# Token scaling one product later, half of FF1's input transposed during the last attention block, and a fourth raw place for W1

## The chip, the core and the metric

The kernel runs on one core of one Trainium2 chip. The metric is the device time of one execution in microseconds (us). Its five engines work from queues of their own, each in its program's order: TensorE (PE, matrix products and transposes; PEld is its weight load), VectorE (DVE), ScalarE (ACT), GpSimd (POOL) and SyncE (SP), whose queue issues nearly all DMA transfers. They wait for each other by semaphores.

## The reference

One layer of a decoder trunk on x of 2048 tokens x 1024, all in float32:

```python
a = rms_norm(h, pre_mix_g)
z = a @ w_in                  # 2568 columns: q | k | v | forget logits | u | v_sg
y_att = forgetting_attention(q, k, v, f + f_bias)      # 8 heads of 64, causal
y_sg = chunked_spatial_gating(u_sg, v_sg, ...)         # chunks of 128, 8 groups
y = concat([rms_norm(y_att, att_out_g), rms_norm(y_sg, sg_out_g)])
h = h + rms_norm(y @ w_out, post_mix_g)
c = rms_norm(h, pre_ffn_g)
ff = square(relu(c @ w_ff1)) @ w_ff2                   # 1024 -> 4096 -> 1024
h = h + rms_norm(ff, post_ffn_g)
h = h + sigmoid(h @ ple_gate_w + ple_gate_b) * (p @ ple_w)
```

`rms_norm(x, g)` divides each token by the root of its mean square and multiplies by a gain.

## The kernel before

**Products.** A float32 operand is kept as two parts, a rounded high part and the rest. `mm3` (L102 to L104) makes one product of them from three matrix instructions. ACT writes the high part (`wsp`, `w1p`, `B`: a cast, or an evacuation with a scale, L114), DVE or POOL the low part (L98, L115, L1011). So each operand passes ACT, then DVE or POOL, then PE.

**Input projection** (0 to about 545 us). The tokens are worked in four blocks of 512 (`block(b)`, L346). A block has 24 products: six groups of columns (`GROUPS`) times four. The first three groups give the forget logits, u and v_sg (accumulator `pacc`, evacuated by ACT to `zf` and `ug`, L374, L375), the last three q, k, v (evacuated to `stg`). Behind product number i the `hooks[i]` are called: they load and norm the next block's x. `x_norm` (L292) takes the squares of four token tiles (L303), on POOL the root (L109), and scales x by it (L314). `x_turn` (L316) transposes the scaled x by tiles of 128, one of eight column tiles (kc) behind each of the products 15 to 22, and writes the left operands (`wide`).

**Attention** (about 545 to 1102 us). Blocks b of 512 queries, eight heads in each, so 16 steps per head in the last block b=3, which begins at about 850 us. A step is a pair of score products (L660, L662), the weights on ACT and DVE (`pr`, `hl`), and three products with V (L685 to L687). Between the steps, at rates per step (`Spread`), the output projection of the block before is done (`project(b)`): yT times W_out, the norm of z (L756 to L760), plus x (L763), and the store of the new h into `hS` in DRAM (L764). `hr_all` receives the root for FF1's norm (L771, L772).

**Last projection** (1102 to 1165 us). `project(3)`, four token tiles tt with two halves of 24 products each. Between the products FF1's first input is made: a tile of h (four token tiles times 128 columns, 256 KB) is loaded from `hS` (L1029), multiplied by `hr_all` on POOL (L1030), transposed on PE (L1035), scaled by the gain on ACT. Such tiles go through four places: `v`, `x`, and `ws` twice, called ws0 and ws1 here, plus `px`. `turn` (L1038) stores eight of them to `cS` in DRAM; `join_now` (L1069) joins eight others straight into FF1's right operands `B`. `prep_first` (L1101) strings both together as 16 steps, which a `Filler` spreads over 54 of the projection's ticks; later `join_load` and `join` fetch the stored ones and join them.

**FF1** (1165 to about 1820 us) multiplies by a scheme with seven products of sums of quarter matrices (m = 1 to 7). It runs in units u of 256 columns. `load_w1` (L1131) loads a half unit of W1 (512 KB) into one of three raw places `w1raw`, and `left` (L1182) makes each left operand `w1p` from it: a sum on DVE (L1195, `ws` once more), a cast on ACT (L1008), the low part on DVE (L1011). In `left` the next unit's loads are called for at n = 3 and n = 5 of the seven. The results are stored as `hidC` (L1219). About 1300 us the right operands of the second half are made as well (`prep_next`, `pxn`), stored to `jS` and read back as `B<-jS` at about 1508 us.

**FF2 and the gate** run to the end.

SP's queue works in order. A transfer stands behind each earlier one that still waits: behind `hS<-z` until DVE has made z, behind a load until its place is free.

## Time and profile before

| | us |
|---|---|
| median of 3 runs | 2671.08 (2671.01 to 2671.46) |
| the profiled execution's own time | 2670.59 |
| its span in the trace | 2668.8 |
| PE busy | 2602.6 (98%), 12188 instructions |
| DVE busy | 1803.9 (68%) |
| ACT busy | 1357.6 (51%) |
| POOL busy | 847.7 (32%) |
| mean granted TensorE clock | 0.992 |

A share near 98% for PE says that the rest, 66 us, is in single waits, and only a view of these waits by line says where. The granted clock is a factor on PE's speed: where it is 0.5, a product takes twice its time, and PE counts as busy all the while.

### The profile page before, as it was taken

The page shows a single profiled execution, that of the slowest core. Times are in us where ns is not written, and L with a number is a line of the kernel's source. Part 1 is how long each engine was busy: PE and PEld are TensorE (multiplying, and loading weights), DVE is VectorE, ACT ScalarE, POOL GpSimd, SP SyncE. Part 2 cuts the span into 40 slices and gives each one's busy share as a digit, 9 for nine tenths or more (in the row PEclk, how much of TensorE's full clock was granted, in tenths as well). Part 3 has the DMA queues.
Part 4 walks back from the last instruction along what each step waited for, and adds up shares of the span by engine and source line. Part 5 has one row for each costly group of instructions (what it writes and reads, how often), then busy time and mean ns, then how long its engine had stood idle before and what let it go on. Part 6 is the DMA issues. An engine that isn't in the chain of part 4 may idle for free.

```text
span 2668.8 us, 37153 instructions
## 1 busy us (share of the span) xinstructions
PE 2602.6 (98%) x12188; PEld 2107.5 (79%) x12188; DVE 1803.9 (68%) x3047; ACT 1357.6 (51%) x2678; POOL 847.7 (32%) x823
## 2 busy tenths in 40 slices
PE   8999999999999999989999999999999999999999
PEld 8797879766677777768788788888888888888887
DVE  5445576766778665688788676778786696875443
ACT  7444443348877777655455454455435544453111
POOL 5444443511111110343344223236360171401211
PEclk9999999999999999999999999999999999999999
DMA  6566656497988776455655854448466644673331
GB/s 183 159 185 167 189 154 170 137 223 186 224 205 191 171 194 146 130 179 202 203 194 181 305 170 158 146 153 293 123 207 212 197 151 137 214 248 109 111 119 61
DMA packets 440081, 472.59 MB, mean 177 GB/s; under 512 B 155088, under 2 KB 269520, under 8 KB 439888
## 3 DMA queue, kind: packets, MB, share of 16 engines
q1 hardware_dynamic: 429651, 454.16, 57.9%
q10 hardware_dynamic: 10237, 16.07, 2.2%
q8 instruction: 96, 1.57, 0.3%
q14 instruction: 97, 0.79, 0.1%
HBM read 336.28 MB, written 133.82 MB: 176 GB/s over the span
## 4 chain that ended last, share of the span: by engine, by line
PE 52%; DVE 2%; DMA 2%; issue 1%; POOL 1%; ACT 0%; SPq 0%; DVEq 0%; POOLq 0%; ACTq 0%
PE pf L104 17%; PE pf L103 17%; PE pf L102 17%; DMA w1raw<-in_w_ff_dram 2%; PE pf L1497 1%; DVE w1p L1011 1%; DVE ws L1195 0%; POOL hq L1222 0%; DVE B L1011 0%; PE pf L1035 0%; DMA x<-hS 0%; POOL tmp L1087 0%; DVE hq L1214 0%; DMA cS<-ws 0%; DVE z L763 0%
## 5 line engine op out<-in xcount | busy, mean ns | idle before, releaser
L102 PE MATMUL pf<-B,w1p 128*128 128x512 f32 x752 | 298.1, 397 | 5.9 <-ACT w1p L1008 3.9
L104 PE MATMUL pf<-B,w1p 128*128 128x512 f32 x752 | 296.7, 395 | 5.1 <-DVE w1p L1011 5.0
L1222 POOL TENSOR_TENSOR hq<-hq,hq 128x512 f32<-128x512 f32 x128 | 196.1, 1542 | 329.7 <-ACT hq L1216 294.1
L103 PE MATMUL pf<-B,w1p 128*128 128x512 f32 x752 | 297.3, 395 | 0.0
L673 DVE TENSOR_TENSOR hl<-pr,hl 128x512 fp32r<-128x512 f32 (+1 forms) x320 | 193.4, 616 | 101.8 <-ACT hl L672 85.2
L664 ACT ACTIVATE pr<-pS,bias 128x512 f32<-128x512 f32 (+1 forms) x320 | 194.7, 622 | 86.4 <-PE pS L662 81.6
L98 POOL TENSOR_TENSOR wsp<-wraw,wsp 128x344 fp32r<-128x344 f32 (+1 forms) x176 | 193.0, 1130 | 116.4 <-ACT wsp L94 106.7
L102 PE MATMUL pf<-R,L 128*128 128x512 f32 x452 | 175.9, 389 | 0.0
L104 PE MATMUL pf<-R,L 128*128 128x512 f32 x452 | 175.8, 389 | 0.0
L103 PE MATMUL pf<-R,L 128*128 128x512 f32 x452 | 175.8, 389 | 0.0
L104 PEld LDWEIGHTS pf<-B,w1p 128*128 128x128 f32 x752 | 141.9, 189 | 40.9 <-DVE w1p L1011 8.4
L102 PEld LDWEIGHTS pf<-B,w1p 128*128 128x128 f32 x752 | 141.7, 188 | 40.9 <-ACT w1p L1008 4.3
L103 PEld LDWEIGHTS pf<-B,w1p 128*128 128x128 f32 x752 | 141.7, 188 | 31.6
L102 PE MATMUL pacc<-wsp,wide 128*128 128x344 f32 (+1 forms) x480 | 165.0, 344 | 1.5 <-ACT wide L114 1.5
L672 ACT CAST hl<-pr 128x512 fp32r<-128x512 f32 (+3 forms) x272 | 145.4, 548 | 34.7 <-POOL pr L666 31.2
L103 PE MATMUL pacc<-wsp,wide 128*128 128x344 f32 (+1 forms) x480 | 161.6, 337 | 0.0
L104 PE MATMUL pacc<-wsp,wide 128*128 128x344 f32 (+1 forms) x480 | 161.5, 336 | 0.0
L187 DVE TENSOR_REDUCE mx<-pM 128x1 f32<-128x512 f32 x192 | 129.7, 685 | 41.5 <-PE pM L185 40.8
L1008 ACT CAST L<-lr 128x512 fp32r<-128x512 f32 x113 | 70.3, 622 | 149.8 <-PE pf L103 121.4
L1011 DVE TENSOR_TENSOR L<-lr,L 128x512 fp32r<-128x512 f32 x113 | 96.0, 850 | 69.2 <-ACT L L1008 68.8
L1008 ACT CAST w1p<-w1raw 128x512 fp32r<-128x512 f32 (+1 forms) x123 | 73.3, 598 | 128.3 <-PE pf L103 124.1
L1011 DVE TENSOR_TENSOR w1p<-ws,w1p 128x512 fp32r<-128x512 f32 (+1 forms) x136 | 118.7, 877 | 28.1 <-ACT w1p L1008 26.3
(445 smaller groups left out, 7192.7 us busy)
## 6 DMA issues: line engine op xcount, KB each, us to landing
hidC<-hq SPq DMA_DIRECT2D x224, 256.0 KB
lr<-hidC SPq DMA_DIRECT2D x224, 256.0 KB
w1raw<-in_w_ff_dram SPq DMA_DIRECT2D x64, 512.0 KB
w1raw<-in_w_ff_dram SPq DMA_DIRECT2D x128, 256.0 KB
...
```

The lines of the kernel that those rows point to most:

```text
L98: e.tensor_tensor(dst[:, 1], src, dst[:, 0].bitcast(F32), ALU.subtract)
L102: pe.matmul(ps, l[0], r[0], start=first, stop=False)
L103: pe.matmul(ps, l[0], r[1], start=False, stop=False)
L104: pe.matmul(ps, l[1], r[0], start=False, stop=last)
L187: ve.tensor_reduce(mx[:, tt, c:c + 1], ps, AX.X, ALU.max)
L664: sc.activation(pr[:, off:], ps[:, off:], AF.Exp, bias=bias_of(b)[:, j, h:h + 1])
L672: sc.copy(hl[:, 0, off:], pr[:, off:])
L673: ve.tensor_tensor(hl[:, 1, off:], pr[:, off:], hl[:, 0, off:].bitcast(F32), ALU.subtract)
L1008: sc.copy(dst[:, 0], src)
L1011: (po if lo == "pool" else ve).tensor_tensor(dst[:, 1], src, dst[:, 0].bitcast(F32), ALU.subtract)
L1222: po.tensor_tensor(t, x, y, op)
L1497: pe.transpose(ps[:, kk], hts[t][g][:, kk * P:(kk + 1) * P], ident)
```

## The change

It has three parts. Line numbers below are those of the kernel each list belongs to.

**A.** `x_norm` ends with the root, kept per token tile as `xr0` to `xr3`. The scaling is a function of its own, `x_scale`, called behind the next product, and ordered after that product's evacuation (`tc.issue_after`). For the tiles loaded first DVE scales one half, as before.

**B.** `turns(g)` does the eight transpositions that were stored to `cS` (kc = 2, 6, 3, 7 for two groups of 512 tokens) in the last attention block, one step every five of its steps, through one place `hx` and a PSUM bank that the heads use too. `prep_first` is left with `join_now`, which loads one step ahead through `v`, `x`, ws0 and ws1. It has eight counted steps over 36 ticks; what is left is done at once when they are through. The joins of the stored tiles are spread over 24 ticks, one of them (m = 6) later.

**C.** W1 has a fourth raw place, `w1more`, in which two of the stored tiles lie before, and the next unit's loads are called for at n = 0 and n = 2. `px` gets a place of its own.

```diff
--- before.py
+++ after.py
@@ -111,8 +112,9 @@
 
     def evac_split(dst, ps, scale, lo_out=None):
 
-        sc.activation(dst[:, 0], ps, AF.Copy, scale=scale)
+        hi = sc.activation(dst[:, 0], ps, AF.Copy, scale=scale)
         ve.scalar_tensor_tensor(dst[:, 1], ps, scale, dst[:, 0].bitcast(F32), ALU.mult, ALU.subtract)
+        return hi
 
 
     mph = ExitStack()
...
@@ -304,14 +306,18 @@
                                       accum_out=ss[:, tt, hf:hf + 1])
                 n = t1 - t0
                 ve.tensor_tensor(ss[:, t0:t1, 0], ss[:, t0:t1, 0], ss[:, t0:t1, 1], ALU.add)
-                r = rstd_of(small, ss[:, t0:t1, 0], n, D, "xr")
-                for tt in range(t0, t1):
-                    for hf in range(2):
-                        xh, rt = st["xs"][tt][:, hf * 512:(hf + 1) * 512], r[:, tt - t0:tt - t0 + 1]
-                        if rest is not None and not hf:
-                            ve.tensor_scalar(xh, xh, rt, None, ALU.mult)
-                        else:
-                            sc.activation(xh, xh, AF.Copy, scale=rt)
+                r = st["r", t0] = rstd_of(small, ss[:, t0:t1, 0], n, D, f"xr{t0}")
+                if rest is not None:
+                    x_scale(st, t0, True)
+
+        def x_scale(st, tt, first=False):
+            r = st["r", tt]
+            for hf in range(2):
+                xh = st["xs"][tt][:, hf * 512:(hf + 1) * 512]
+                if first and not hf:
+                    ve.tensor_scalar(xh, xh, r, None, ALU.mult)
+                else:
+                    sc.activation(xh, xh, AF.Copy, scale=r)
 
         def x_turn(st, b, kc, aT):
             ps = ptp.tile([P, 4, P], F32, name="tp")
...
@@ -372,17 +378,18 @@
 
             def fu_done(tt, ps):
                 sc.copy(zf[:, tt], ps[:, :H])
-                sc.activation(ug[:, tt, :336], ps[:, H:344], AF.Gelu_apprx_tanh)
+                return sc.activation(ug[:, tt, :336], ps[:, H:344], AF.Gelu_apprx_tanh)
 
             def qk_done(dst, scale):
...
@@ -493,10 +500,13 @@
                         else:
                             mm3(ps[:, :width], (aT[kc][:, 0, ns], aT[kc][:, 1, ns]),
                                 (wt[kc][:, 0, :width], wt[kc][:, 1, :width]), kc == 0, kc == KC - 1)
-                    dones[gi](n, ps)
+                    evac = dones[gi](n, ps)
                     i = 4 * gi + n
                     for f in mine.get(i, ()):
                         f()
+                    for f in behind.get(i, ()):
+                        with tc.issue_after(evac.ins):
+                            f()
                     for f in hooks.get(i, ()):
                         f()
                     if n == 3 and gi + 1 < len(GROUPS):
...
+            nxt, behind = [], {}
             if b + 1 < NB:
                 box = {}
                 hooks[7].append(lambda: box.update(x_load(b + 1)))
                 for tt in range(4):
                     hooks[XN[tt]].append(lambda tt=tt: x_norm(box, ((tt, tt + 1),)))
+                    behind[XN[tt] + 1] = [lambda tt=tt: x_scale(box, tt)]
                 for kc in range(KC):
                     hooks[15 + kc].append(lambda kc=kc: x_turn(box, b + 1, kc, nxt))
-            block(b, aT, hooks, fill, None if b else (ug0, gv0, wt0))
+            block(b, aT, hooks, behind, fill, None if b else (ug0, gv0, wt0))
             if b < NB - 1:
                 fill.drain()
             aT = nxt
...
@@ -824,9 +836,31 @@
             if not last:
                 yield
 
+    def turns(g):
+
+        t0 = g * 4
+        for kc in (2, 6, 3, 7):
+            hx = yp.tile([P, 4, P], F32, name="hx", bufs=1)
+            sy.dma_start(hx, hS[t0 * P:(t0 + 4) * P, kc * P:(kc + 1) * P].rearrange("(a p) c -> p a c", p=P))
+            po.tensor_tensor(hx, hx, hr_all[:, t0:t0 + 4].unsqueeze(2).broadcast_to([P, 4, P]), ALU.mult)
+            yield
+            ps = pT.tile([P, 4, P], F32, name="pT")
+            for a in range(4):
+                pe.transpose(ps[:, a], hx[:, a], ident)
+            hx = hx.rearrange("p a b -> p (a b)")
+            sc.activation(hx, ps.rearrange("p a b -> p (a b)"), AF.Copy, scale=g_pf[:, kc:kc + 1])
+            sy.dma_start(cS[kc, :, g * 512:(g + 1) * 512], hx)
+            yield
+
+    projected = []
+
+    def project_all(b):
+        yield from project(b)
+        projected.append(b)
+
     YSQ, YNO = 8, 13
     YSQL, YNOL = 2, 7
-    PREPT = 54
+    PREPT, JOINT = 36, 24
     GAP = 2
     FIN = (0, 2)
     LA = 4
     LA = 4
@@ -893,6 +927,7 @@
     lv = Spread(late_v())
     mx3 = Spread(fill.gen, maxima(NB - 1))
     proj = Spread()
+    turned = [Spread(turns(g)) for g in range(2)]
     n3 = m_units(NB - 1)
     m01 = (M3PART * n3 + fill.left) / MEND
     rates = {0: (m01, 0), 1: (m01, 0), 2: ((1 - M3PART) * n3 / 94, P2PARTS / 96),
...
@@ -918,6 +953,7 @@
         if i == 24:
             sy.dma_start(g_att, att_out_g[0].partition_broadcast(P))
             sy.dma_start(g_post, post_mix_g[0].partition_broadcast(P))
+            sy.dma_start(g_pf, pre_ffn_g[0].rearrange("(k p) -> p k", p=P))
         for d, f in ((0, load_wo), (WOH, wo_hi), (WOL, wo_lo)):
             if i - d in WO:
                 f(WO[i - d])
...
         proj.tick(rates[b][1])
+        if b == NB - 1:
+            for g in projected:
+                if g < 2:
+                    turned[g].tick(.2)
     for _ in late[1]:
         pass
+    for t in turned:
+        t.drain()
     aph.close()
     mph.close()
 
...
@@ -970,22 +1012,21 @@
     w1s = ExitStack()
     w1q = pool(w1s, "w1q", side="right")
     pf1 = pool(fps, "pf1", 3, PSUM, side="right")
-    g_pf = per_part(fsm, "g_pf", pre_ffn_g, KC)
     v_t = fsm.tile([P, 512], F32, name="v")
     x_t = fsm.tile([P, 512], F32, name="x")
     ng_pf = fsm.tile([P, KC], F32, name="ng_pf")
     ve.tensor_scalar(ng_pf, g_pf, -1.0, None, ALU.mult)
     ws = [fsm.tile([P, 4, P], F32, name=f"ws{e}") for e in range(2)]
-    px = [*ws, w1q.tile([P, 4, P], F32, name="px")]
 
     def w1_places(pl):
 
         all = pl.tile([P, 3, KC, P], F32, name="w1raw")
-        return all, [all[:, e] for e in range(3)]
+        return all, [all[:, 2], all[:, 0], all[:, 1], w1more]
 
     def w1_pieces(pl):
         return [pl.tile([P, 2, 4, P], F32R, name=f"w1p{e}") for e in range(3)]
 
+    w1more = fsm.tile([P, KC, P], F32, name="w1more")
     _, w1raw = w1_places(w1q)
     w1p = w1_pieces(w1q)
 
@@ -993,7 +1034,7 @@
 
     LATE = (6, 3, 7, 2, 4)
     B = [[None] * KH for _ in range(8)]
-    EARLY = (1, 3, 2, 5, 6)
+    EARLY = (1, 3, 2, 5)
     early = [ctx3.tile([P, 2, 512], F32R, name=f"B{m}_2") for m in EARLY]
     kept = [ctx3.tile([P, 2, 512], F32R, name=f"B{m}_1") for m in LATE]
     for k in range(2):
...
@@ -1066,13 +1097,24 @@
             halves_of(B[m][k], t, "act", "dve")
             yield
 
-    def join_now(k, b, place, done, ra, rd, h1, h2):
+    def join_now(k, b, place, done, ra, rd, hs):
+
 
         t2 = None
-        for n, (hx, dst, jh, l) in enumerate(((h1, ra, 0, 0), (h2, rd, 1, 1), (h1, None, 0, 1), (h2, None, 1, 0))):
+        ahead = len(hs) > 1
+        parts = ((ra, 0, 0), (rd, 1, 1), (None, 0, 1), (None, 1, 0))
+
+        def fetched(n):
+            if n < 4:
+                normed(hs[n % len(hs)], KH * parts[n][1] + k, 2 * b + parts[n][2])
+
+        if ahead:
+            fetched(0)
+        for n, (dst, jh, l) in enumerate(parts):
+            hx = hs[n % len(hs)]
             kc = KH * jh + k
             g, ng = g_pf[:, kc:kc + 1], ng_pf[:, kc:kc + 1]
-            normed(hx, kc, 2 * b + l)
+            fetched(n + ahead)
             yield
             ps = turned(hx)
             if n < 2:
@@ -1099,18 +1141,10 @@
 
 
     def prep_first():
-        pa = w1raw[0].rearrange("p k f -> p (k f)")
-        pb = w1raw[1].rearrange("p k f -> p (k f)")
+        pa = w1raw[1].rearrange("p k f -> p (k f)")
         v4, x4 = (t.rearrange("p (a b) -> p a b", b=P) for t in (v_t, x_t))
-        n = 0
         for k in range(2):
-            now = join_now(k, 0, lambda m: B[m][k], lambda m: None, pa[:, :512], pa[:, 512:], v4, x4)
-            for g in range(2):
-                for kc in (2 + k, 6 + k):
-                    for _ in turn(kc, g, px[n % 3]):
-                        next(now)
-                        yield
-                    n += 1
+            yield from join_now(k, 0, lambda m: B[m][k], lambda m: None, pa[:, :512], pa[:, 512:], [v4, x4, *ws])
 
     def prep_next():
 
...
+
+    pxn = px = None
+    raws, nraw, nleft = {}, 0, 0
     lefts = {}
 
     def load_w1(u, c):
         nonlocal nraw
-        t = w1raw[nraw % 3]
+        t = w1raw[nraw % 4]
         nraw += 1
         f0 = u % NF * FCH + c * P
         sy.dma_start(t, w_ff1[:, f0:f0 + P].rearrange("(k p) f -> p k f", p=P))
         raws[u, c] = t
 
     load_w1(0, 0)
-    pfill = Filler(prep_first(), 16, PREPT)
-    w1raw1 = w1raw[1].rearrange("p k f -> p (k f)")
-    jraw = [w1raw1[:, :512], w1raw1[:, 512:], v_t, px[2].rearrange("p a b -> p (a b)")]
+    pfill = Filler(prep_first(), 8, PREPT)
+    w1raw1 = w1raw[2].rearrange("p k f -> p (k f)")
+    w1more1 = w1more.rearrange("p k f -> p (k f)")
+    jraw = [w1raw1[:, :512], w1raw1[:, 512:], w1more1[:, :512], w1more1[:, 512:]]
     pl = []
     join2 = None
     for n, _ in enumerate(last_proj):
@@ -1147,9 +1182,9 @@
         if not pfill.left and join2 is None:
             pfill.drain()
             join_load(2, jraw)
-            pl += [new_tmp() for _ in range(2)]
+            pl.append(new_tmp())
             join2 = join(2, lambda: pl.pop(0), jraw)
-            jfill = Filler(join2, 5, 10)
+            jfill = Filler(join2, len(EARLY), JOINT)
         elif join2 is not None:
             jfill.tick()
     while jfill.left:
@@ -1200,9 +1235,9 @@
         halves_of(w[:, :, kk], t, "act", "dve")
         lefts[i] = w
         if u + 1 < NU and ks[-1] == 3:
-            if n == 3:
+            if n == 0:
                 load_w1(u + 1, 0)
-            elif n == 5:
+            elif n == 2:
                 load_w1(u + 1, 1)
 
     hq = {}
...
@@ -1382,7 +1418,7 @@
     fill = Filler(prep_next(), 32, 13 * 7)
     jrest = join_rest()
     hold = first_of[NF + 2]
-    JR = (1, 1, 2, 2, 1, 1, 1)
+    JR = (1, 1, 2, 2, 2, 1, 1)
 
     NEXT = [[(1, 2), (1, 3)], [(5, 2), (5, 3)], [(6, 1)], [(3, 1), (6, 2), (6, 3)], [(7, 1), (3, 2), (3, 3)],
             [(2, 1), (7, 2), (7, 3)], [(4, 1), (2, 2), (2, 3), (4, 2), (4, 3)]]
```

`normed` and `turned` are unchanged, but the name `turned` is also that of the list of the two spread generators. ACT in the first block's products (`pacc` to `zf` and `ug`), before:

```order
L303 ACTIVATE junk,xss<-xt 128x512 x5
L374 COPY zf<-pacc 128x8
L375 ACTIVATE ug<-pacc 128x336
L314 ACTIVATE xt<-xt,xr 128x512 x6
L374 COPY zf<-pacc 128x8
L375 ACTIVATE ug<-pacc 128x336
L94 CAST wsp<-wraw 128x512 x4
```

and with the change:

```order
L305 ACTIVATE junk,xss<-xt 128x512
L380 COPY zf<-pacc 128x8
L381 ACTIVATE ug<-pacc 128x336
L95 CAST wsp<-wraw 128x512 x6
L380 COPY zf<-pacc 128x8
L381 ACTIVATE ug<-pacc 128x336
L95 CAST wsp<-wraw 128x512
L402 ACT_TABLE_LOAD
L402 ACTIVATE lse<-lse 128x32
L95 CAST wsp<-wraw 128x512
L115 ACTIVATE stg<-pacc 128x512
L320 ACTIVATE xt<-xt,xr_883 128x512 x2
```

The six scalings that stood ahead of an evacuation now go in pairs, each behind an evacuation to `stg`.

PE where the last projection's third token tile (tile 2) begins, with `pT<-ident,yn` as the mark of that place, before:

```order
L1035 MATMUL pf_12619<-ident,ws_12326 128x128 x4
L1035 MATMUL pf_12626<-ident,v 128x128 x4
L102 MATMUL pM<-wide_118,yaT 128x512
L103 MATMUL pM<-wide_118,yaT 128x512
L104 MATMUL pM<-wide_118,yaT 128x512
L102 MATMUL pM<-wide_120,yaT 128x512
L103 MATMUL pM<-wide_120,yaT 128x512
L104 MATMUL pM<-wide_120,yaT 128x512
L781 MATMUL pT<-ident,yn 128x128 x4
```

and with the change (ws_12405 is ws0, ws_12406 is ws1):

```order
L1076 MATMUL pf_12657<-ident,ws_12406 128x128 x4
L1076 MATMUL pf_12672<-ident,v 128x128 x4
L1076 MATMUL pf_12682<-ident,x 128x128 x4
L793 MATMUL pT<-ident,yn 128x128 x4
L103 MATMUL pW<-wide_126,ysT 128x512
L1076 MATMUL pf_12692<-ident,ws_12405 128x128 x4
L104 MATMUL pW<-wide_126,ysT 128x512
L105 MATMUL pW<-wide_126,ysT 128x512
L103 MATMUL pW<-wide_128,ysT 128x512
L104 MATMUL pW<-wide_128,ysT 128x512
L105 MATMUL pW<-wide_128,ysT 128x512
L1076 MATMUL pf_12709<-ident,ws_12406 128x128 x4
```

SP's queue ahead of it, with the change:

```order
L1070 DMA v<-hS 128x4x128
L741 DMA ysT<-ysS 128x1024
L1070 DMA x<-hS 128x4x128
L776 DMA hS<-z_12512 128x512
L776 DMA hS<-z_12536 128x512
L819 DMA xt_12596<-in_x_dram 128x512
L819 DMA xt_12621<-in_x_dram 128x512
L1070 DMA ws_12405<-hS 128x4x128
L741 DMA ysT<-ysS 128x1024
L1070 DMA ws_12406<-hS 128x4x128
```

The steps that were spread through two token tiles stand close together at the third's start, and ws1 is used twice within it.

SP in the last attention block, where the fourth of the new tiles is loaded, before:

```order
L637 DMA KA<-kS 64x4x512
L639 DMA V<-vS 128x16x64 x2
L707 DMA attS<-yo 128x4x64
L764 DMA hS<-z_10447 128x512
L764 DMA hS<-z_10575 128x512
L807 DMA xt_10722<-in_x_dram 128x512
```

and with the change:

```order
L649 DMA KA<-kS 64x4x512
L852 DMA cS<-hx 128x512
L651 DMA V<-vS 128x16x64 x2
L719 DMA attS<-yo 128x4x64
L776 DMA hS<-z_10469 128x512
L844 DMA hx<-hS 128x4x128
L776 DMA hS<-z_10600 128x512
```

The store of one tile and the load of the next stand among the loads of the heads; this load is behind one of the two stores of z.

More of the change, by code (lines that the diff above doesn't have):

```diff
@@ L67, in trunk @@
     hr_all = const.tile([P, NT], F32, name="hr_all")
+    g_pf = const.tile([P, KC], F32, name="g_pf")
     mix_stack = ExitStack()
@@ L344, in trunk, with block @@
         GROUPS = ((2224, 344), (1880, 344), (1536, 344), (0, 512), (512, 512), (1024, 512))
-        def block(b, aT, hooks, fill, first=None):
+        def block(b, aT, hooks, behind, fill, first=None):
             ug, gv, wt = first or (sg1.tile([P, 4, AW], F32, name="ug"), sg1.tile([P, 4, AW], F32, name="gv"), None)
@@ L524, in trunk @@
                 for i in range(2):
-                    hooks[i] += [lambda i=i: x_norm(st, ((2 + i, 3 + i),)), lambda i=i: x_turn_tile(st, 2 + i, wide)]
+                    hooks[i] += [lambda i=i: x_norm(st, ((2 + i, 3 + i),)), lambda i=i: x_scale(st, 2 + i, True),
+                                 lambda i=i: x_turn_tile(st, 2 + i, wide)]
                 hooks[SGW].append(prep_sgw)
             fill = Filler(maxima(b - 1), m_units(b - 1), (23 if b < NB - 1 else MT) * KC) if b else Filler(iter(()), 0, 1)
-            nxt = []
+            nxt, behind = [], {}
             if b + 1 < NB:
@@ L1036, in turned @@
         return ps
-    def turn(kc, g, hx):
-        normed(hx, kc, g)
-        yield
-        ps = turned(hx)
-        hx = hx.rearrange("p a b -> p (a b)")
-        sc.activation(hx, ps, AF.Copy, scale=g_pf[:, kc:kc + 1])
-        sy.dma_start(cS[kc, :, g * 512:(g + 1) * 512], hx)
-        yield
     def join_load(k, raws):
@@ L1123, in done @@
                     sy.dma_start(jS[m - 1, k - 1], place(m).bitcast(F32))
-            yield from join_now(k, 1, place, done, *pxn, px[2], px[2])
-    pxn = None
-    raws, nraw, nleft = {}, 2, 0
+            yield from join_now(k, 1, place, done, *pxn, [px])
+    pxn = px = None
+    raws, nraw, nleft = {}, 0, 0
     lefts = {}
@@ L1396, in trunk @@
             pxn = [hqp.tile([P, 512], F32, name=f"pxn{e}") for e in range(2)]
+            px = hqp.tile([P, 4, P], F32, name="px")
             for t in ((0, 0), (0, 1), (1, 0), (1, 1), 5, 6):
```

11 lines of the change are left out of this document (6 added, 5 removed).

## The prediction

> **What bounds the kernel now.** I read the page's busy shares first, then TensorE's waits, then the windows around the longest waits.
>
> ```profile
> PE 2602.6 (98%) x12188; PEld 2107.5 (79%) x12188; DVE 1803.9 (68%) x3047; ACT 1357.6 (51%) x2678; POOL 847.7 (32%) x823
> ...
> PE 52%; DVE 2%; DMA 2%; issue 1%; POOL 1%; ACT 0%; SPq 0%; DVEq 0%; POOLq 0%; ACTq 0%
> ```
>
> PE (TensorE) works for 2602.6 of 2668.8 us, so all its idle time together is 66.2 us. The change takes no matrix product away; it can gain only from those 66 us and from stretches where the products run at a lower granted clock. The waits say which idle time it can reach:
>
> ```profile
> PE pacc L102 <- ACT ug L375: 6.7, 2, 4.7
> PE pf L102 <- ACT w1p L1008: 5.9, 2, 3.9
> PE pf L1035 <- POOL x L1030: 5.8, 1, 5.8
> PE pf L104 <- DVE w1p L1011: 5.1, 6, 2.7
> PE pf L102 <- DMA B<-jS: 2.0, 5, 0.5
> ```
>
> The columns are total, times, longest. The first row belongs to the split scaling (A), the third to the moved transposes (B), the last two to the fourth W1 place (C); the second is divided between B (3.88) and C (2.01). The windows below (PE busy is the first number behind the length, then come the other engines, PEclk, DMA share) show that long waits cost twice:
>
> ```profile
> 68.00:74.00 6.00, 5.86 (x14) 4.61 (x15) 2.95 (x5) 3.70 (x10) 5.33 (x5) 0.50 0.37 93
> 200.00:204.00 4.00, 3.61 (x9) 2.91 (x10) 0.83 (x6) 4.00 (x10) 3.19 (x5) 0.57 0.12 22
> 1050.00:1100.00 50.00, 49.96 (x235) 36.55 (x233) 28.59 (x56) 36.17 (x71) 6.83 (x11) 1.00 0.43 108
> 1141.00:1146.00 5.00, 4.81 (x14) 3.96 (x15) 4.32 (x6) 1.92 (x4) 4.25 (x6) 0.51 0.69 228
> 1176.00:1180.00 4.00, 3.63 (x8) 2.45 (x9) 4.00 (x11) 1.91 (x5) 1.91 (x1) 0.58 0.59 195
> 1316.00:1320.00 4.00, 3.89 (x10) 3.06 (x11) 4.00 (x7) 2.43 (x4) 1.28 (x1) 0.57 0.82 316
> ```
>
> I price a slow stretch as PE's busy time times (1 - PEclk): 5.86 x 0.50 = 2.9 us, 3.61 x 0.43 = 1.55, 4.81 x 0.49 = 2.4, 3.63 x 0.42 = 1.5, 3.89 x 0.43 = 1.7.
>
> [...]
>
> **Part A, the scaling one product later.** The chain at 57 to 68 us:
>
> ```profile
> 63.91 3.78 ACT L314 ACTIVATE xt<-xt,xr 128x512 f32<-128x512 f32 x6 [6.65 <-POOL xr L109]
> 67.64 0.44 ACT L375 ACTIVATE ug<-pacc 128x336 f32<-128x336 f32 x1
> ...
> 68.14 0.79 PE L102 MATMUL pacc<-wide,wsp 128*128 128x512 f32 x1 [4.70 <-ACT ug L375]
> ...
> 200.39 0.79 PE L102 MATMUL pacc<-wide,wsp 128*128 128x512 f32 x1 [2.04 <-ACT ug L375]
> ```
>
> ACT executes in order. It stood idle 6.65 us for the root of the squares, then did six scalings in 3.78 us, and only then the evacuation that frees PE's accumulator. With the change the evacuations (zf, ug) stand ahead of the scalings in ACT's order, so both waits and their slow stretches go: 4.70 + 2.9 + 2.04 + 1.55 = 11.2 us. Nothing is added: the same eight scalings per block run later. What can be late next is the transposition that reads them: the fourth of its four transposes stands behind two products (0.21 us each, 49.96 / 235) and three half as wide, about 1 us with the three transposes, while the last tile's evacuation (0.69 for such a tile, quoted at 1142.35) and first scaling (0.63, 3.78 / 6) take 1.3. I take 0.3 us a block for three blocks, 1 in all, between 0 and 1.5. **A: -10.2**, from -9.7 to -11.2.
>
> **Part B, eight of the sixteen transpositions in attention.** What they cause in the last projection, with SP's queue in order:
>
> ```profile
> 1130.21 0.93 SPq L764 DMA_DIRECT2D hS<-z  x2
> 1131.19 0.95 SPq L807 DMA_DIRECT2D xt<-in_x_dram  x2
> ...
> 1133.90 0.50 SPq L1029 DMA_DIRECT2D x<-hS  x1
> ...
> 1140.10 1.04 POOL L1030 TENSOR_TENSOR x<-x,hr_all 128x512 f32<-128x512 f32 x1 [3.66 <-DMA x<-hS]
> ...
> 1141.19 1.12 PE L1035 MATMUL pf<-ident,x 128*128 128x128 f32 x4 [5.82 <-POOL x L1030]
> ```
>
> The reload of x stands behind the store of z, which waits for VectorE (DVE), and lands 6.2 us after its issue. This exact wait goes, since fewer tiles pass the four places: 5.82 + 2.4 = 8.2 us. But the order shows a new meeting where PE begins tile 2: ws1 is transposed there and wanted again, refilled, 16 transposes and six products later. The reload may start only when the first transposes are done. Its price from these rows:
>
> ```profile
> 1131.50 0.66 PE L781 MATMUL pT<-ident,yn 128*128 128x128 f32 x4 [0.35 <-DVE yn L725]
> ...
> 1111.86 0.36 SPq L1029 DMA_DIRECT2D ws<-hS  x1
> ...
> 1114.91 1.04 POOL L1030 TENSOR_TENSOR ws<-ws,hr_all 128x512 f32<-128x512 f32 x1 [1.17 <-DMA ws<-hS]
> ```
>
> A reload takes 3.05 us (1111.86 to 1114.91) to 6.2 before POOL starts, plus 1.04, plus 0.4 for the issue: 4.5 to 7.6. The cover is 16 transposes at up to 0.66 / 4 and six products at 0.21 (49.96 / 235 above): 3.2 to 3.9. So PE waits 0.6 to 4.4. Ahead of it the reload of ws0 stands in SP's queue behind the same two stores and two xt loads as x did; it is wanted 1.3 us sooner, but DVE does z straight after its root now, with no join between, so I add little. I take 2.8 for both and a third of a slow stretch of 2.4, 0.8: +3.6, bounds 0 and 8.2.
>
> The wait where FF1 starts:
>
> ```profile
> 1142.35 0.69 ACT L1079 ACTIVATE w1raw<-pf,g_pf 128x512 f32<-128x512 f32 x1 [3.70 <-PE pf L1035]
> ...
> 1175.23 0.63 ACT L766 ACTIVATE yjunk<-z 128x512 f32<-128x512 f32 x1 [3.85 <-DVE z L763]
> ...
> 1176.30 0.54 PE L102 MATMUL pf<-B,w1p 128*128 128x512 f32 x1 [3.88 <-ACT w1p L1008]
> ```
>
> The last two rows cost 3.88 + 1.5 = 5.4. The cast that PE waits for stands behind yjunk on ACT, which waits for DVE's z. Both orders have it so; only the joins that slow DVE there are spread thinner. I take -1, between -5.4 and 0.
>
> In attention come eight loads, POOL products (1.04 us each), groups of four transposes, ACT copies (0.69, as at 1142.35) and stores. PE has no gap there (49.96 of 50 above), so the transposes lengthen attention by what they shorten the projection: zero. ACT has 14 and POOL 43 idle us of 50 as cover for 0.69 and 1.04 every 80 to 90 products (18 us at 0.21). DVE has 21 idle us. The costly thing is a late tile, since PE's order is fixed and there is one hx place. Placing each group by its neighbours in the order, I find 5 us or more of slack for all but two; the tightest is the fourth, whose load stands right behind the first of these stores, and whose transposes come after the 472nd of the 640 score products (L660 and L662), here at 955.73:
>
> ```profile
> 949.02 0.99 SPq L764 DMA_DIRECT2D hS<-z  x2
> ...
> 955.73 0.40 PE L662 MATMUL pS<-QB,KA 128*128 128x512 f32 x1
> ...
> SPq L764 <- DVE z L763: 42.6, 5, 11.6
> ```
>
> From 949.5 on, 3.05 to 6.2 and 1.04 us end at 953.6 to 956.7: up to 1 us late. I take +1 for attention, between 0 and one stall like x's, 8.2.
>
> [...]
>
> **B: -8.2 + 3.6 - 1 + 1 = -4.6.**
>
> **Part C, the fourth place.**
>
> ```profile
> 1303.33 2.55 SPq L1136 DMA_DIRECT2D w1raw<-in_w_ff_dram  x2
> ...
> 1308.33 0.69 DVE L1195 TENSOR_TENSOR ws<-w1raw 128x512 f32<-128x512 f32 x1 [2.85 <-DMA w1raw<-in_w_ff_dram]
> ...
> 1301.56 0.50 PE L104 MATMUL pf<-B,w1p 128*128 128x512 f32 x1 [0.65 <-DVE w1p L1011]
> 1316.11 0.50 PE L104 MATMUL pf<-B,w1p 128*128 128x512 f32 x1 [2.68 <-DVE w1p L1011]
> ...
> 1512.09 0.41 ACT L1008 CAST w1p<-w1raw 128x256 fp32r<-128x256 f32 x1 [1.62 <-PE pf L103]
> ...
> 1522.45 0.51 PE L102 MATMUL pf<-C,w1p 128*128 128x512 f32 x1 [2.01 <-ACT w1p L1008]
> ```
>
> In SP's order the loads keep their place behind the stores of the unit, so they cannot start earlier than about 1301.8; only the wait for a free place goes. That brings the first load 1.5 us and the second more forward, of the 2.85 that DVE waited. I take 1.8 of the 2.68, and the slow stretch of 1.7, since what is left is under 1 us: 3.5. The 0.65 is no load's doing. Near 1512 to 1522 the five B<-jS waits (2.0) and the 2.01 come from a burst (five B<-jS, three w1raw) from which one load leaves: 1.3 of 4.0 is my estimate. The other small waits of that row (5.1 - 2.68 - 0.65 = 1.8): 0.4. **C: -5.2**, from -1.3 (only the burst) to -10.8 (5.1 + 1.7 + 4.0).
>
> **Sum.** -10.2 - 4.6 - 5.2 = -20.0. The profiled execution took 2670.6 (1.8 over its span), so 2650.6; the median lies 0.5 above it: **2651 us**.
>
> **Rivals.**
> 1. *The reloads wait as long as x did.* For it: same queue, same stores, and a place refilled only after its own transposes. Against: DVE has less ahead of z, and the refill may take 3 us. B then loses 8.2 - 3.6 = 4.6: 2656.
> 2. *The fourth place brings nothing,* since DVE, busy 4.00 of 4.00 us at 1316, sets FF1's pace and the SP order is the old one: 5.2 less, 2656.
> 3. *FF1's start is cured too* and the reloads cost 1 us only, because transfers land in 3 us and DVE's z comes early: 4.4 + 2.6 more, 2644.
> 4. *Slower: late hx tiles.* SP stands up to 11.6 us behind z in attention and each late tile costs a stall and a slow stretch like x's, 8.2. Without my 1 us the sum is 2650; two or three late tiles make 2666 to 2675, no change; from four on it is slower, 2683. Against: six slacks of 5 us.
>
> **How the numbers follow.** Forecast 0.48; rivals 1: 0.15, 2: 0.13, 3: 0.12, 4 with two or three tiles: 0.07, with four: 0.05. About 0.2% (5.3 us) is what a measurement can tell, so faster 0.88, no change 0.07, slower 0.05. The forecast's own range is 2645 to 2658; for 8 in 10 I take 2640, where C's far end leads, to 2664, where rivals 1 and 2 come together (2661) with an hx tile half late.
>
> **What would show it.** A: no wait on ug over 1 us and PEclk 1.00 at 68 and 200 us; if one stays, A is wrong. B: no wait on x; a wait on ws at the start of tile 2, 0.6 to 4.4 us; one on w1p at FF1's start of 3 us. Attention: waits on hx of 1 us in all; several of 5 us make the prediction wrong. C: the 2.68 below 1 us and PEclk 1.00 there; the B<-jS waits still over 1 us.

## The result

The changed kernel takes **2648.19 us** (median of 4 runs, 2644.02 to 2650.82) where the kernel before takes 2671.05 beside it: 22.9 us less, a ratio of 0.9912 with a 95% interval of 0.9900 to 0.9924. The forecast was 2651, the range 2640 to 2664. The profiled execution took 2644.02 us, with a span of 2642.3, the quickest of the four.

The page of the changed kernel, part 1 and the first line of part 4:

```profile
PE 2591.2 (98%) x12188; PEld 2097.4 (79%) x12188; DVE 1835.0 (69%) x3049; ACT 1360.0 (51%) x2676; POOL 852.5 (32%) x823
...
PE 56%; DMA 1%; DVE 1%; issue 0%; POOL 0%; ACT 0%; SPq 0%; DVEq 0%; POOLq 0%
```

PE is idle for 51.1 us of the span instead of 66.2, and busy 11.4 us less with the same 12188 instructions. So the gain in this execution, 26.5 us of span, is 15 us of waits and 11 us of clock. TensorE's waits with the change:

```profile
PE pacc L103 <- DVE stg L116: 5.9, 2, 3.4
PE pf L103 <- ACT w1p L1049: 4.3, 2, 2.3
PE pf L1076 <- POOL ws L1071: 1.9, 2, 1.2
PE pf L103 <- DMA B<-jS: 1.6, 5, 0.5
PE tp L325 <- ACT xt L320: 0.5, 1, 0.5
PE pf L105 <- DVE w1p L1052: 0.3, 1, 0.3
```

Against the rows of before: the waits on ug (6.7 us) and on x (5.8) are gone, those of L105 on DVE's w1p fell from 5.1 to 0.3. The first row grew: two waits on the low part of `stg`, up to 3.4 us, where before has three, up to 1.7:

```profile
PE pacc L102 <- DVE stg L115: 4.1, 3, 1.7
```

The windows that were slow before, and PE's rows of the waits that are left:

```profile
68.00:74.00 6.00, 5.43 (x23) 3.79 (x22) 2.76 (x1) 4.36 (x7) 6.00 (x6) 1.00 0.80 209
200.00:204.00 4.00, 3.93 (x17) 3.22 (x18) 3.86 (x5) 2.34 (x4) 4.00 (x5) 1.00 0.77 201
1141.00:1146.00 5.00, 5.00 (x24) 4.14 (x23) 4.97 (x12) 2.50 (x6) 2.21 (x2) 1.00 0.59 210
1316.00:1320.00 4.00, 4.00 (x21) 3.28 (x20) 3.93 (x4) 1.79 (x3) 1.84 (x2) 1.00 0.63 240
```

```profile
79.69 0.50 PE L103 MATMUL pacc<-wide,wsp 128*128 128x512 f32 x1 [3.45 <-DVE stg L116]
208.92 0.50 PE L103 MATMUL pacc<-wide,wsp 128*128 128x512 f32 x1 [2.42 <-DVE stg L116]
```

To see where the time went I set each matrix product of the one trace beside its counterpart in the other and took the difference of their starts (median over 10 us of program, good to about 0.8 us). Negative is earlier than before:

| place in the program, us of the kernel before | the change | the change, a second profile |
|---|---|---|
| 75, behind the first wait on ug | -6.4 | -6.3 |
| 85, behind the first wait on stg | -4.1 | -4.0 |
| 205, behind the second wait on ug | -7.9 | -6.9 |
| 370, third block | -7.9 | -6.0 |
| 510, end of the input projection | -9.0 | -6.6 |
| 590 | -11.2 | -5.6 |
| 720, first heads of attention | -13.9 | -3.1 |
| 1040, the eight new groups of transposes are through | -10.9 | +0.3 |
| 1125 | -12.8 | -2.0 |
| 1135 | -11.0 | -1.4 |
| 1145, behind the old wait on x | -17.2 | -7.4 |
| 1210, FF1 under way | -21.2 | -11.6 |
| 1320, behind the old wait in FF1 | -26.7 | -17.1 |
| 1510 | -27.2 | -17.1 |

From 720 us on the two profiles of the same kernel agree: -13.3 and -14.0 more. Up to there they differ by 10.8 us. The first experiment is about that.

### The profile page after: what moved, and what is told of

Read it like the earlier page. It is cut to its first block, busy times and chain, and to the rows that moved or that the text cites. A ratio compares the mean times of both kernels' runs of the same rounds, so it can differ in the third digit from the quotient of the medians.

```text
span 2642.3 us, 37186 instructions
## 1 busy us (share of the span) xinstructions
PE 2591.2 (98%) x12188; PEld 2097.4 (79%) x12188; DVE 1835.0 (69%) x3049; ACT 1360.0 (51%) x2676; POOL 852.5 (32%) x823
## 4 chain that ended last, share of the span: by engine, by line
PE 56%; DMA 1%; DVE 1%; issue 0%; POOL 0%; ACT 0%; SPq 0%; DVEq 0%; POOLq 0%
PE pf L105 18%; PE pf L104 18%; PE pf L103 18%; PE pf L1534 1%; DMA B<-jS 1%; DMA w1more<-in_w_ff_dram 0%; PE pf L1076 0%; PE pM L105 0%; PE pM L103 0%; PE pM L104 0%; PE pW L105 0%; DMA ws<-hS 0%; PE pW L104 0%; PE pW L103 0%; DVE B L1052 0%
## 5 line engine op out<-in xcount | busy, mean ns | idle before, releaser
L105 PE MATMUL pf<-B,w1p 128*128 128x512 f32 x752 | 295.9, 394 | 0.4 <-DVE w1p L1052 0.3
L105 PE MATMUL pf<-R,L 128*128 128x512 f32 x452 | 175.8, 389 | 0.0
L105 PEld LDWEIGHTS pf<-B,w1p 128*128 128x128 f32 x752 | 141.8, 189 | 34.5 <-DVE w1p L1052 1.6
L684 ACT CAST hl<-pr 128x512 fp32r<-128x512 f32 (+3 forms) x272 | 145.4, 548 | 34.2 <-POOL pr L678 30.9
L105 PE MATMUL pacc<-wsp,wide 128*128 128x344 f32 (+1 forms) x480 | 161.1, 336 | 0.0
L1052 DVE TENSOR_TENSOR w1p<-ws,w1p 128x512 fp32r<-128x512 f32 (+1 forms) x136 | 124.7, 917 | 12.8 <-ACT w1p L1049 12.2
L187 PE MATMUL pM<-KM,QM 128*128 128x512 f32 (+2 forms) x320 | 117.7, 372 | 9.0 <-DVE mx L189 7.6
```

The source lines that it names most:

```text
L105: pe.matmul(ps, l[1], r[0], start=False, stop=last)
L187: pe.matmul(ps[:, :w], q[:, tt * P:(tt + 1) * P], km[:, :w], start=True, stop=True)
L684: sc.copy(hl[:, 0, off:], pr[:, off:])
L1052: (po if lo == "pool" else ve).tensor_tensor(dst[:, 1], src, dst[:, 0].bitcast(F32), ALU.subtract)
```

## The experiments

For every kernel the median of its runs and of the runs of the kernel before on the same chip, the ratio with its interval, and from its one profile PE's idle time (the sum of the waits that its timeline shows) and the clock lost (the sum of PE's busy time times 1 - PEclk over windows of 4 us):

| kernel | us | before | ratio | idle | clock lost |
|---|---|---|---|---|---|
| before | | 2671.05 | 1 | 58.8 | 15.8 |
| the change | 2648.19 | 2671.05 | 0.9912 (0.9900 to 0.9924) | 43.1 | 4.4 |
| the change again | 2648.44 | 2669.7 | 0.9918 (0.9904 to 0.9932) | 45.7 | 13.8 |
| A alone | 2658.67 | 2669.7 | 0.9957 (0.9946 to 0.9969) | 51.3 | 13.1 |
| B and C | 2658.49 | 2669.7 | 0.9956 (0.9943 to 0.9968) | 49.4 | 12.5 |
| B alone | 2661.96 | 2669.7 | 0.9967 (0.9956 to 0.9979) | 54.3 | 12.3 |
| A and B | 2654.12 | 2668.03 | 0.9946 (0.9933 to 0.9958) | 46.7 | 11.1 |
| late calls, four places | 2647.24 | 2669.21 | 0.9918 (0.9903 to 0.9933) | 43.2 | 5.9 |
| chain behind stg | 2639.99 | 2668.03 | 0.9894 (0.9881 to 0.9907) | 38.5 | 7.4 |
| every other low part of q on DVE | 2640.19 | 2669.21 | 0.9896 (0.9881 to 0.9911) | 39.8 | 6.2 |
| joins on DVE | 2645.47 | 2668.03 | 0.9919 (0.9905 to 0.9932) | 43.5 | 6.3 |
| chain behind stg, joins on DVE | 2637.29 | 2668.03 | 0.9886 (0.9873 to 0.9898) | 34.2 | 12.9 |
| all three | 2635.54 | 2669.21 | 0.9876 (0.9857 to 0.9895) | 37.1 | 7.0 |

The median of the kernel before differs from one set of runs to the next (2668.03 to 2671.05), so kernels with different values of before are better compared by their ratios, where 0.001 is 2.7 us.

### The change once more

No edit.

> The changed kernel once more, unedited. Theory 1 (the slow clock that follows a wait of about 2 us is a matter of chance): its times spread over 2644 to 2651 again, and in its profile slow stretches stand behind other waits than in the first one, where only the waits of 2.25 us at 1156 and of 2.01 at 1494 had them; the 4.7 us gained at the start of attention (580 to 700 us) come and go. Theory 2 (the clock follows from the wait's length alone): the same waits are followed by the same PEclk, and the start of attention shows no slow stretch again.

Measured: 2648.44 us, runs from 2643.36 to 2653.32. Its profile is of the slowest of them, 9.3 us longer in span than the first profile. Windows of the first profile, behind waits of the kernel:

```profile
80.00:84.00 4.00, 4.00 (x19) 3.20 (x18) 0.69 (x1) 1.82 (x3) 0.00 (x0) 1.00 0.79 228
572.00:576.00 4.00, 3.08 (x12) 1.86 (x13) 2.15 (x4) 2.17 (x4) 0.00 (x0) 1.00 0.87 223
704.00:708.00 4.00, 3.33 (x18) 2.34 (x17) 3.07 (x6) 3.07 (x7) 0.57 (x1) 1.00 0.63 213
```

and of the second:

```profile
80.00:84.00 4.00, 4.00 (x12) 3.16 (x11) 0.69 (x1) 1.82 (x3) 0.00 (x0) 0.57 0.85 222
576.00:580.00 4.00, 4.00 (x9) 2.73 (x10) 1.55 (x3) 2.01 (x4) 0.00 (x0) 0.50 1.10 242
712.00:716.00 4.00, 3.97 (x10) 3.19 (x11) 1.90 (x4) 2.27 (x5) 0.57 (x1) 0.57 0.76 279
```

In the first profile the wait at 79 us lasted 3.45 us and no slow stretch followed. In the second it lasted 2.62, and one followed: 12 products in 4 us instead of 19. Three more kernels have this wait unchanged: 2.62 us with PEclk 1.00 behind it in two of them (A and B; late calls), 2.60 with 0.57 in the third (joins on DVE). So theory 1 holds: whether a slow stretch follows a wait of 2 to 3.5 us is not set by its length alone. One costs 1.5 to 3 us by PE's busy time times (1 - PEclk): 4.00 x 0.43 = 1.7 in the second profile's row at 80, 1.5 to 2.9 in the windows of the kernel before. The 4.7 us at the start of attention belong to no part of the change.

The traces also show how often. Each trace keeps the start and length of every stretch at half clock. In that of the kernel before they start at 9.26, 67.29, 200.41, 582.70, 685.10, 1139.07, 1176.62 and 1316.57 us: the later ones 17, 56, 168, 198, 331, 342 and 383 steps of 3.41 us behind the first. They last 3.41 or 6.83 us, one step or two (a PEclk of 0.57 over 4 us is one step); only the one at the program's end (6.07 us) is no whole number of steps. In that of the change they start at 9.83, 1156.71 and 1494.63 us, 336 and 435 steps behind the first, and last 3.41 us each. All 13 profiles of this document have such a grid. It lies differently against the program in each execution: a step of the change begins at 78.10 us in the first profile, at 77.19 in the second. I counted how long PE is idle within each step at full clock between 12 and 2620 us, and whether the step behind it is at half clock. In the 13 profiles it is behind all 41 steps with 1.9 us or more of idle time, behind none of the 9660 with less than 0.95, and behind 18 of the 148 between; in the kernel before alone behind 6 of 6, 0 of 735 and 1 of 12, in the change's first profile 2 of 2, 0 of 744 and 0 of 15. Here are the steps about the wait at 79 us, in the first profile and in the second:

```profile
74.68:78.10 3.42, 1.56 (x7) 0.94 (x5) 2.98 (x14) 0.00 (x0) 0.43 (x1) 1.00 0.83 218
78.10:81.51 3.41, 1.82 (x8) 1.51 (x9) 2.34 (x9) 1.34 (x3) 0.00 (x0) 1.00 0.39 116
```

```profile
77.19:80.60 3.41, 1.46 (x6) 1.23 (x7) 1.94 (x10) 0.08 (x1) 0.00 (x0) 1.00 0.46 152
80.60:84.01 3.41, 3.41 (x9) 2.64 (x9) 0.69 (x1) 1.73 (x3) 0.00 (x0) 0.50 0.87 234
```

The wait of 3.45 us is cut by a border of the grid into 1.86 and 1.59, and the clock stays. The wait of 2.62 lies with 1.95 in one step, and the next step runs at half clock.

### A alone, and the change without A

The edit of the first is the change's hunks on `evac_split`, `x_norm`, `x_scale`, `fu_done`, `qk_done` and `behind`, put on the kernel before; the second takes the same hunks out of the change:

```diff
-                for tt in range(t0, t1):
-                    for hf in range(2):
...
-                            sc.activation(xh, xh, AF.Copy, scale=rt)
+                    behind[XN[tt] + 1] = [lambda tt=tt: x_scale(box, tt)]
```

> The kernel before with part A alone. Theory 1: A gains what the trace shows up to 370 us, 8 us, so 2663; the waits on ug are gone, and waits on the low part of stg of about 3.4 and 2.4 us stand in their place. Theory 2: A also sets how attention starts, so the 4.7 us from 580 to 700 us belong to it: 2658. My prediction had 10.2 for A: 2661.

> The change with part A undone (B and C stay). Theory 1: 8 us more than the change, about 2656, with waits on ug of 4.7 and 2.0 us as before. Theory 2: 12.7 more, 2661.

Measured: A alone 2658.67, 11.0 us under before; without A 2658.49, 10.0 us over the change on the same chip. Theory 1 said 8 and theory 2 12.7; both lie about as far off, and the profiles decide. A alone has slow stretches at 572 to 580 and 676 to 684 us, where the kernel before has its own, so the start of attention was not what it gained. TensorE's waits with A alone:

```profile
PE pacc L102 <- DVE stg L115: 4.8, 2, 2.4
PE pS L671 <- DMA QS<-qS: 3.0, 2, 2.1
```

and without A:

```profile
PE pacc L103 <- ACT ug L376: 6.7, 2, 4.7
PE pacc L103 <- DVE stg L116: 6.7, 3, 2.6
```

The waits on ug come and go with A. The longer waits on stg do not: without A they last 2.56, 2.40 and 1.72 us, with B alone 2.67, 2.39 and 1.25. The kernel before has 1.42, 0.97 and 1.74, and the clock accounts for that. The first wait on stg, before and without A:

```profile
83.74 0.50 PE L102 MATMUL pacc<-wide,wsp 128*128 128x512 f32 x1 [1.42 <-DVE stg L115]
```

```profile
84.36 0.51 PE L103 MATMUL pacc<-wide,wsp 128*128 128x512 f32 x1 [2.56 <-DVE stg L116]
```

From the end of the wait on ug to the end of this wait PE takes 15.60 us in the kernel before, and 15.61 without A and with B alone. Yet behind the wait on ug the first runs 6.0 us at half clock, the other two 3.4. At the second pair of waits it is 14.66, 14.64 and 14.63 us, with 3.4 us at half clock before and none in the other two. So DVE's low part of stg sets when PE goes on, and a slow stretch ahead of this wait costs nothing up to there.

Between A alone and before PE's idle time differs by 7.5 us (58.8 to 51.3). PE's busy time differs by 3.5 with the same instructions, which I put down to the clock (the sums over windows give 2.7); together they make up the 11.0.

### B alone

A undone as above, and C undone:

```diff
-        t = w1raw[nraw % 4]
+        t = w1raw[nraw % 3]
-            if n == 0:
+            if n == 3:
-            elif n == 2:
+            elif n == 5:
```

> The kernel before with part B alone (A undone; C undone: three raw places, loads called for at n = 3 and 5). The lag between the two traces grows by 7.3 us from 720 to 1290 us, where B acts, with 3.1 us lost in attention and 10.4 gained after it. Theory 1: 2664, the wait of 2.68 us in FF1 still there. My prediction had 4.6 for B: 2666.5. Rival: parts do not add, since the waits in FF1 depend on where FF1 starts: then this is over 3 us from 2664.

Measured: 2661.96, 7.7 us under before, the 7.3 of the traces within the spread, and the wait in FF1 is still there (2.59 us at 1308). My 4.6 was too small. A, B and C as taken alone or away (11.0, 7.7 and the 5.7 below) make 24.4 against 21.3 and 22.9 for all: they add, as well as such runs can tell.

### A and B, and the late calls

The first is the change with the edit just shown; the second keeps `nraw % 4` and sets only n to 3 and 5.

> The change with part C undone: W1 rotates through three places again, loads called for at n = 3 and 5. In the order, the calls at n = 3 and 5 with four places give SP nearly the same row of loads as n = 0 and 2, so what C does is the fourth place alone. By the lag between the traces of before and after, C is worth 4.5 us at 1316, 0.9 at 1301 and about 1 after 1400: 5 to 6.5 us more than the change, with a wait on w1p of 2 to 3 us and PEclk near 0.57 at about 1290 to 1300. My prediction had 5.2. Rival, from the three runs' medians (2669.7 less 11.0 for A, less 7.7 for B, against 2648.4): C is worth 2.6 only.

> The change, with the next unit's W1 loads called for at n = 3 and 5 as before, but four places. In the order SP's row of loads differs in one place of FF1 only. Theory: the fourth place does all of C's work, so the time is the change's, 2645 to 2651, and no wait on w1p of over 1 us stands near 1290 to 1300 us. Rival: the earlier calls matter, and the time is that of the kernel with C undone, 6 us more, with the wait of 2.4 us back.

Measured: A and B 2654.12, 5.7 us over the change; the ratios, 0.9946 and 0.9918, make 7.5. By matched products, from 1145 to 1600 us A and B lose 5.9 and 6.1 us on the two profiles of the change. Late calls: 2647.24, the change's own time. TensorE's waits of A and B:

```profile
PE pf L105 <- DVE w1p L1052: 4.0, 4, 2.4
```

and with late calls:

```profile
PE pf L105 <- DVE w1p L1052: 1.8, 2, 1.4
PE pf L103 <- ACT w1p L1049: 3.2, 2, 2.0
```

With three places the wait of 2.4 us at 1299.5 us is back; with four it is gone, whatever the calls. The 1.4 of the late calls stands at FF1's start, where it and one of 1.2 take the place of the change's 2.25. The fourth place does the work of C; "loaded sooner" comes from it and not from the calls. The rival of 2.6 falls by the matched products; the intervals of the ratios alone would just allow it.

### The chain of the forget gates, and what holds it

The wait on stg is the longest that the change leaves, and my prediction did not have it. DVE and POOL of the changed kernel there, POOL's row first:

```profile
65.06 10.05 POOL L99 TENSOR_TENSOR wsp<-wraw,wsp 128x512 fp32r<-128x512 f32 x8
```

```profile
71.24 3.91 DVE L403 TENSOR_SCALAR lss<-lse 128x32 f32<-128x32 f32 x1 [7.20 <-ACT lse L402]
...
78.95 0.68 DVE L116 SCALAR_TENSOR_TENSOR stg<-pacc,stg 128x512 fp32r<-128x512 f32 x1
```

DVE's operation on 128 x 32 numbers takes 3.91 us and ends with POOL's row of eight, at 75.1. The low part of stg, for which PE's accumulator waits, stands behind the whole chain. Two experiments, on the place of the chain and on POOL's row. The first calls `log_sigmoid` behind product 12's low part (`lows` collects those instructions):

```diff
+                    if i == 12 and b < NB - 1:
+                        with tc.issue_after(lows[-1].ins):
+                            log_sigmoid()
```

> The change, with the log-sigmoid chain of the forget gates put behind the low part of product 12's evacuation on DVE, where the change has it ahead of it. Theory L (POOL's row of eight wsp products, 65.06 to 75.11 us, holds DVE's first operation on lse for 3.91 us, and the low part of stg stands behind it): the waits of 3.45 and 2.42 us on stg are gone or under 1 us, the chain's first operation still ends where POOL's row ends, and the time is 4 to 6 us shorter. Rival (the operation is late because ACT's table load and sigmoid are late): they are later still here, and the waits on stg stay or go to the next product.

The second leaves the chain and shortens the row:

```diff
-                      lo="dve" if raws and kc in LO_DVE else "pool")
+                      lo="dve" if raws and kc in LO_DVE or c0 == 0 and kc % 2 else "pool")
```

> The change, with every other low part of the q weights (the group of 512 columns whose eight wsp products make POOL's row from 65 to 75 us) made on DVE instead of POOL. The log-sigmoid chain keeps its place ahead of stg's low part. Theory L (POOL's row holds DVE's operation on lse): the row is half as long, the operation that took 3.91 us takes at most one POOL product, 1.3 us, the wait of 3.45 us on stg falls under 1.5, and the time is 2 to 5 us shorter than the change. Rival (the chain is late because of ACT's sigmoid, which comes at 70.98 us in the change): the operation and the wait stay as they are.

Measured: 2639.99 and 2640.19, both 8 us under the change's medians; those are of other chips, and by the ratios it is 4.3 to 6.4 us. DVE with the chain moved:

```profile
71.96 0.69 DVE L118 SCALAR_TENSOR_TENSOR stg<-pacc,stg 128x512 fp32r<-128x512 f32 x1 [8.19 <-ACT stg L117]
...
72.83 1.30 DVE L415 COPY car<-csum 128x8 f32<-128x8 f32 x1
74.04 1.36 DVE L403 SCALAR_TENSOR_TENSOR lse<-zf 128x32 f32<-128x32 f32 x1
```

and DVE, POOL and PE with the row shortened:

```profile
71.14 0.18 DVE L403 TENSOR_SCALAR lss<-lse 128x32 f32<-128x32 f32 x1 [2.35 <-ACT lse L402]
```

```profile
64.96 6.29 POOL L99 TENSOR_TENSOR wsp<-wraw,wsp 128x512 fp32r<-128x512 f32 x5
71.70 1.29 POOL L99 TENSOR_TENSOR wsp<-wraw,wsp 128x512 fp32r<-128x512 f32 x1 [0.45 <-ACT wsp L95]
```

```profile
76.97 0.50 PE L103 MATMUL pacc<-wide,wsp 128*128 128x512 f32 x1 [1.55 <-DVE stg L116]
```

With the chain moved, no wait on stg is left in the list. So what PE waited for was a low part that stood behind the chain. My detail that the chain's first operation would end with POOL's row was wrong: the two small operations of the rows above took 1.30 and 1.36 us.

With the row shortened, ACT's sigmoid comes at the same time (70.88 us after 70.98), yet the chain is done 2.7 us sooner: the rival falls, and POOL's row is shown to lengthen the chain. The row fell from eight products to six, not to half, and the waits are 1.55 and 1.79 us, a little over the 1.5 expected. The operation that took 3.91 us takes 0.18, but this alone proves little. With A alone, beside a row of all eight products, it takes 0.18 as well, and operations behind it lose the time:

```profile
71.26 0.18 DVE L402 TENSOR_SCALAR lss<-lse 128x32 f32<-128x32 f32 x1 [7.16 <-ACT lse L401]
...
72.72 1.22 DVE L405 TENSOR_TENSOR lss<-lss 128x32 f32<-128x32 f32 x1
73.97 1.20 DVE L406 TENSOR_SCALAR lpl<-lss 128x32 f32<-128x32 f32 x1
```

What holds is the whole chain, from this operation to the low part of stg: 7.7 and 6.8 us in the two profiles of the change, 6.7 with A alone, 5.1 with the row shortened. In the kernel before it is 6.5, as seven operations of the chain take 4.65 us beside POOL where the change has 1.55. So the chain, the row and the wait met there already.

By matched products the moved chain gives 3.7 us at 80 and 2.7 at 210. The sum, 6.4, is what the ratios of 0.9894 and 0.9918 make.

One POOL product of the row takes 1.26 us (10.05 / 8). The small operations of 1.20 to 1.36 us took about as long as one of them, the one of 3.91 us as three. Why it took three is not shown.

### The joins on DVE

At FF1's start DVE and POOL of the changed kernel:

```profile
1150.15 2.81 DVE L772 SCALAR_TENSOR_TENSOR z<-z,zr,g_post 128x512 f32<-128x512 f32 x2 [0.44 <-POOL zr L769]
1152.88 2.36 DVE L775 TENSOR_TENSOR z<-z,xt 128x512 f32<-128x512 f32 x2
```

```profile
1150.73 3.35 POOL L1096 TENSOR_TENSOR j<-r,r 128x512 f32<-128x512 f32 x2
```

```diff
-        for m, e in ((5, po), (6, ve), (7, po), (4, ve)):
+        for m, e in ((5, ve), (6, ve), (7, ve), (4, ve)):
```

> The change, with the two subtractions per join that POOL does done on DVE. At 1150 us POOL's two subtractions (3.35 us) stand beside DVE's two scalings of z (2.81 us for two, 1.48 where POOL rests) and two sums (2.36 for two, 1.36). Theory L: DVE's z is ready 2.3 us sooner, the wait on w1p at FF1's start falls from 2.25 to under 1.5, and no slow stretch follows it: 1 to 4 us shorter. Rival (DVE is simply full there): two more operations of 0.69 make z later, the wait grows to 3 us.

Measured: 2645.47, 3.0 us under the change's second median, with runs from 2643.89 to 2652.78; the intervals of the ratios (0.9905 to 0.9932, 0.9904 to 0.9932) are the same, so the time alone shows nothing. The timeline does. DVE and PE with this edit:

```profile
1153.17 1.76 DVE L772 SCALAR_TENSOR_TENSOR z<-z,zr,g_post 128x512 f32<-128x512 f32 x2 [0.44 <-POOL zr L769]
1154.86 1.28 DVE L775 TENSOR_TENSOR z<-z,xt 128x512 f32<-128x512 f32 x2
```

```profile
1156.70 0.50 PE L103 MATMUL pf<-B,w1p 128*128 128x512 f32 x1 [0.54 <-ACT w1p L1049]
```

DVE's z takes 3.04 us instead of 5.17, and PE's first wait in FF1 falls from 2.25 to 0.54. But 2 us come back within 20 us (0.49 on DVE's w1p at 1161.2 and 1.69 at 1175.9), where DVE is busy for 19.97 of 20 us: the stall is moved on, not paid off.

### The edits together

> Both of these edits. Theory L: they act in stages far apart and add up, 5 to 9 us shorter than the change, about 2641 where the kernel before has 2670.

> The three edits together: the chain behind product 12's low part, all join subtractions on DVE, every other q low part on DVE. Theory L: the chain no longer stands ahead of anything that PE waits for, so the third edit adds nothing to the other two but shorter waits of PE on wsp (four of 0.28 us at 67 to 70): 2636 to 2638, 1 us under the two alone at most.

Measured: 2637.29 for the chain moved and the joins on DVE, 2635.54 for all three. The last beats both kernels: 33.7 us under the kernel before and, by the ratios (0.9876 against 0.9912 and 0.9918), 9.6 to 11.2 under the change. I expected 2636 to 2638. The first two make 6.9 to 8.5 by the ratios, of the 5 to 9 expected. That the third edit adds 1.7 us is not beyond the spread.

## Why the prediction was right, point by point

**The time** was 3 us off, and all three parts gained. The reading that carried it was the first: with PE at 98%, only named waits and the clock could give anything. That it came so close is in part luck: B gave 3 us more than forecast, and A, by the matched products at 370 us, 1.5 to 4.2 less.

**A, -10.2 forecast, 10.0 and 11.0 measured.** Both waits on ug are gone. The transposes that I priced at 1 us wait 0.5 (the row on `tp L325`). What failed is the price of the slow stretches, 2.9 + 1.55. Behind both of them PE waits for DVE's low part of stg, in the kernel before too, and that wait ends when DVE is done. Without A and with B alone PE has 2.6 us less at half clock behind the first wait on ug and 3.4 less behind the second, and gains nothing by it. "Nothing is added" failed as well. At 75 us PE is 6.4 us earlier than before, but ACT's sigmoid, with which the chain begins, only 5.3 (70.98 after 76.25), and in the first profile the chain takes 1.2 us longer. So the first wait on stg grew from 1.42 to 3.45 us (2.62 in the second profile), and only 4.1 of the 6.4 are left at 85 us. The second wait grew from 0.97 to 2.4; the third, 1.74, is gone. I had looked at what reads the moved scalings and not at PE's next wait on the same accumulator, which stands in the full list of waits before. At 370 us the two profiles of the change are 6.0 and 7.9 us ahead of before, that of A alone 8.7. That the runs show 10 to 11 is clock that A alone lost less of, 13.1 against 15.8 us in one profile each, which is no proof: the match with my 10.2 is partly luck.

**B, -4.6 forecast, 7.7 measured.** The wait on x is gone as said (-6.2 and -6.0 from 1135 to 1145 us in the two profiles). The reloads cost less than my 2.8 and 0.8. PE with the change:

```profile
1120.69 0.66 PE L1076 MATMUL pf<-ident,ws 128*128 128x128 f32 x4 [1.22 <-POOL ws L1071]
1123.23 0.66 PE L1076 MATMUL pf<-ident,ws 128*128 128x128 f32 x4 [0.72 <-POOL ws L1071]
```

1.94 us and no slow stretch in any profile there. The larger wait is the one on ws0, for which I had added little: its reload took 4.85 us from SP's issue to POOL (1114.74 to 1119.59). That of ws1 took at most 3.81 (1117.95 to 1121.76), near the short end of my 3.05 to 6.2. At FF1's start 2.25 us remain of 3.88, 1.6 gained where I took 1. In attention no wait on hx stands in the list, so my 1 us there was too much, and rival 4 did not come about. The transposes lengthen attention by 3.0 us (from 720 to 1040 us: -13.9 to -10.9; 3.4 in the second profile). What they shorten in the projection does not show apart from the waits there. Window of attention with the change:

```profile
895.00:1050.00 155.00, 154.69 (x746) 115.04 (x745) 93.83 (x183) 116.42 (x225) 27.46 (x44) 1.00 0.79 198
```

PE idles 0.3 us in 155, so the seven of POOL's eight products that lie in this window cost nothing there. Where POOL's products beside DVE's work did cost was the chain at 71 us (7.7 us, 5.1 with the row shortened), a stage where I had not looked for it.

**C, -5.2 forecast, 5.7 (7.5 by the ratios) measured.** The 2.68 us are gone altogether, not by 1.8, and a wait of 0.93 that I had left among the small ones with them. The 0.65, which I had called no load's doing, is gone too, but also with A and B alone, so it is not C's. The burst at 1480 to 1494 us gave 0.4 instead of 1.3: the B<-jS waits are 1.6 after 2.0, and the row below is as before.

```profile
1494.13 0.50 PE L103 MATMUL pf<-C,w1p 128*128 128x512 f32 x1 [2.01 <-ACT w1p L1049]
```

The change of the calls to n = 0 and 2 adds nothing, as the unmoved rows in SP's order had let me expect.

**The slow stretches** were priced as sure to go with their waits. They are not sure to come, since a wait can fall across a border of the 3.41 us grid, as the one of 3.45 us at 79 us did (1.86 and 1.59 us, PEclk 1.00 behind it), and where another wait stands behind them they cost nothing (15.60 us up to that wait with 6.0 us at half clock, 15.61 with 3.4): this is the term whose kind was wrong, though the sum bore it. Runs of the changed kernel spread over 7 to 10 us. The kernel before spreads over 7.7 and 8.4 us in two sets of 11 runs, so that the 3 runs I had of it lay within 0.5 was luck.
